# Preparing a scan block for two heads at once, with ScalarE placing the halves

## The chip, the core and the metric

The kernel runs on one core of a Trainium2 chip. Five engines work from their own instruction queues, each in order: TensorE (PE; its weight loads are PEld), VectorE (DVE), ScalarE (ACT), GpSimd (POOL) and SyncE (SP), which here issues all the DMAs. The metric is the time of one execution in device microseconds; before the change the median of three runs is 2986.44 us (2984.91 to 2988.6).

## The reference

The computation is three transformer layers in a row on one sequence of 512 tokens with 1024 channels, all in float32: neighbourhood attention with a gated convolution and an MLP, then a layer with RWKV-7 time mixing between two half-weighted SwiGLU blocks, then one with sliding-window attention between two more of them. The change touches only the RWKV-7 part, whose core is a recurrence over time, for each of 16 heads of 64 channels:

```
def step(S, inp):
    r_t, w_t, k_t, v_t, kk_t, b_t = inp
    sa = einsum('bhij,bhj->bhi', S, -kk_t)
    S = (S * w_t[:, :, None, :] + sa[..., None] * b_t[:, :, None, :]
         + v_t[..., None] * k_t[:, :, None, :])
    y = einsum('bhij,bhj->bhi', S, r_t)
    return S, y
```

Here kk is a normalised key, b = kk * a, and w the decay. The result y is normalised per head, gated and multiplied by an output matrix (w_o).

## The kernel before, in words

**Matrix products.** Every weight chunk of 128x1024 numbers is loaded by `wload` (line 406): a DMA on SP into a raw tile (wr, 3 buffers), a ScalarE copy to a rounded high part (wh, 5 buffers), and a subtraction on VectorE or GpSimd for the low part (wl, 5 buffers). TensorE multiplies three times: high by high, high by low, low by high. These products write PSUM tiles m; everything that runs beside them writes PSUM tiles t.

**The time-mixing part.** The tokens go in two halves, hf = 0 and 1. For each half the mixed inputs are multiplied in the order K (w_k), W, A (small matrices), R (w_r), V (w_v), G (small matrices), all of half 0 first, then of half 1. So the second w_k, w_r and w_v below are those of half 1. The results are spilled to DRAM.

**The scan.** The recurrence is cut into blocks of 128 tokens (j = 0 to 3, two chunks of 64 each), and the heads into two groups of eight, q = 0 and 1. Such a group lies as four pairs of heads in 128 partitions: head e = 0 of a pair in partitions 0 to 63, e = 1 in 64 to 127. For each of the 8 (q, j) there is a `prep(q, j)` (line 1358): it fetches five tiles from DRAM, builds the products of r and kk with the decay (tiles E, one for each e) and those of b and k with its inverse (tile bk), multiplies them on TensorE into small triangular matrices, and sends these (tile F) to DRAM (fsc). When both q of a block are prepared, `inverse(j)` (line 1451) reads them back (iat) and inverts them on GpSimd: 31 steps of a multiply and an add, one after the other (rows h<-a,iat and a<-a,h). The result is written to DRAM (xsc, line 1480) and read back, TensorE finishes the inverse with 32x32 products, and `scan_task(q)` (line 1577) runs the two chunks of the block. `gn_task` (line 1531) normalises a finished block, and `w_o(hf)` (line 1698) may start when both blocks of a half are normalised for both q: `em.until(lambda: min(done["z"]) >= 2 * hf + 1)`.

**What sets the order.** A planner, the class `_Emit`, keeps an estimated clock of every engine and runs these tasks as Python generators: each `yield` names tiles to wait for, and the task goes on when the estimate says that they are ready. So the program order on every engine follows from the estimates, and an instruction more or less moves those after it. A prep starts when at most one other is unfinished and when `room(12)` finds 12 free activation tiles of 56 (line 1524). SP issues its DMAs in this order too, and one that waits holds up those behind it.

**Lines.** The trace puts nearly all vector work on line 290 (292 where it is urgent), products on 379 and transposes on 393, so tile names tell it apart: a is an activation tile, h a half tile, s a small one, cst the constants, sv a state tile of the scan.

Of the kernel before, what the change touches and what calls it, by code (L numbers as in the profile page):

```python
# [297 lines left out]
def tile_net(ctx: ExitStack, tc: tile.TileContext, a: dict, out: bass.AP, dbg=None, stop=None):  # L298
# [13 lines left out]
    def nm(s):  # L312
        uid[0] += 1
        return f"{s}{uid[0]}"
# [3 lines left out]
    def A(dt=F32):  # L318
        live[0] += 1
        peak[0] = max(peak[0], live[0])  # L320
        t_ = apool.tile([P, T], dt, tag="a", name=nm("a"))
        em.new(t_, "a")
        return t_

    def free(*tiles, n=0):

        live[0] -= len(tiles) + n
        em.free(tiles, n)

    def room(n):  # L330
        return live[0] + n <= NA

    def S():
        return spool.tile([P, 64], F32, tag="s", name=nm("s"))

    def H():
        return HX()[:, 0:256]
# [4 lines left out]
    def PS(side=None):  # L342

        tag = "t" if (em.inside if side is None else side) else "m"
        t_ = psum.tile([P, T], F32, tag=tag, name=nm(tag), bufs=BANKS[tag])
        em.new(t_, tag)
        return t_
# [6 lines left out]
    vt, gp, act = _Engine(em, tc, nc.vector, "vt"), _Engine(em, tc, nc.gpsimd, "gp"), _Engine(em, tc, nc.scalar, "act")  # L354
    dma = _Engine(em, tc, nc.sync, "sync").dma_start
    MUL, ADD, SUB, MAX = ALU.mult, ALU.add, ALU.subtract, ALU.max
# [15 lines left out]
    def V(name, i=0):  # L372
        c = _VEC[name] + i
        return vec[:, c : c + 1]
# [3 lines left out]
    def mm(out_, lhsT, rhs, start=True, stop=True):  # L378
        nc.tensor.matmul(out_, lhsT=lhsT, rhs=rhs, start=start, stop=stop)  # L379
        n = 1  # L380
        for d in rhs.shape[1:]:
            n *= d
        m = lhsT.shape[-1]
        dur = 0.0134 * (1 if rhs.dtype == F32R else 2) + (max(n, 2 * m if m > 64 else m) if rhs.dtype == F32R else n * 4) / 2400.0
        em.pe(out_, [lhsT, rhs], em.tile_time(out_, lhsT, dur))
# [11 lines left out]
    def tt(eng, out_, in0, in1, op):  # L397
        eng.tensor_tensor(out=out_, in0=in0, in1=in1, op=op)

    def copy(out_, in_, scale=None):  # L400
        if scale is None:
            act.activation(out=out_, in_=in_, func=AF.Copy)
        else:
            act.activation(out=out_, in_=in_, func=AF.Copy, scale=scale)
# [76 lines left out]
    class Stat:  # L481
# [50 lines left out]
        def all(self):  # L532
            return self.ready[0] and self.ready[1]
# [28 lines left out]
    t_ = H()  # L562
# [76 lines left out]
    for j in range(4):  # L639
        t_ = A()  # L640
# [4 lines left out]
    for g in (1, 3, 5):  # L645
        t_ = A()
# [59 lines left out]
    with tc.tile_pool(name="bpool", bufs=4) as bias_p:  # L706
# [4 lines left out]
        for i in range(4):  # L711
            pc, ph = PS(), PS()
            gemm(pc, a["w_conv"], 3 * i, (0, 8), xs)
            t_ = A()
# [30 lines left out]
    for n in range(DC):  # L745
        sg = []
        for m in range(2):
            ps = PS()
            gemm(ps, a["w_gate"], 8 * m + n, (0, 8), xs)
            t_ = A()  # L750
# [11 lines left out]
        t_ = A()  # L762
# [3 lines left out]
    for c in range(DC):  # L766
        t_ = A()
# [317 lines left out]
    def fetch(src):  # L1085
        t_ = A()
        dma(out=t_, in_=src)
        return t_

    def fetch_q(d, q, j):  # L1090

        t_ = A()
        dma(out=t_.rearrange("p (q t) -> p q t", q=4),
                          in_=d[j // 2][4 * q : 4 * q + 4, :, (j % 2) * 128 : (j % 2 + 1) * 128].rearrange("q p t -> p q t"))
        return t_

    def rwkv(on_h):
# [245 lines left out]
        E, ARB, BKN, TT, PC, F = {}, {}, {}, {}, {}, {}  # L1343
# [14 lines left out]
        def prep(q, j):  # L1358
            kk, aa = fetch(kkd[q, j]), fetch_q(ad, q, j)
            k_, lg, r_ = fetch(kd_[q, j]), fetch(lgd[q, j]), fetch_q(rd, q, j)  # L1360
            yield [kk, aa]

            b_, k2 = A(), aa
            vt.scalar_tensor_tensor(out=b_, in0=kk, scalar=-1.0, in1=aa, op0=MUL, op1=MUL)
            for p in range(4):
                ps_ = slice(p * 128, (p + 1) * 128)
                act.activation(out=k2[:, ps_], in_=aa[:, ps_], func=AF.Identity, scale=V("k_a", 4 * q + p),
                               bias=oka[:, 4 * q + p : 4 * q + p + 1])
            tt(vt, k2, k2, k_, MUL)
            free(k_)  # L1370
            yield [lg, r_]
            ip, pp_ = A(), lg
            act.activation(out=ip, in_=lg, func=AF.Exp, scale=-1.0)
            act.activation(out=pp_, in_=lg, func=AF.Exp)
            pc = S()
            PC[q, j] = pc
            vt.tensor_copy(pc[:, 0:8].rearrange("p (q c) -> p q c", q=4),
                           pp_.rearrange("p (q c t) -> p q c t", q=4, c=2)[:, :, :, 63])

            def tv(t_, pr, c, x0=0, x1=64):  # L1380
                return t_.rearrange("p (q c t) -> p q c t", q=4, c=2)[pr, :, c, x0:x1]

            ff, rb_t = A(), A()
            F[q, j], ARB[q, j] = ff, rb_t
            f4 = ff.rearrange("p (c q f) -> p c q f", c=2, q=4)
            rb4 = rb_t.rearrange("p (c q f) -> p c q f", c=2, q=4)
            for c in range(2):
                bk, cg = A(), 2 * j + c
                b4 = bk.rearrange("p (q f) -> p q f", q=4)
                for e in range(2):  # L1390
                    pr = slice(64 * e, 64 * e + 64)
                    ee = A()
                    E[q, e, cg] = ee
                    e4 = ee.rearrange("p (q f) -> p q f", q=4)
                    tt(vt, e4[pr, :, 64:128], tv(r_, pr, c), tv(pp_, pr, c), MUL)
                    tt(vt, e4[pr, :, 1:64], tv(kk, pr, c, 1, 64), tv(pp_, pr, c, 0, 63), MUL)
                    copy(e4[pr, :, 0:1], tv(kk, pr, c, 0, 1))
                    ob, ok = (0, 64) if e == 0 else (64, 0)
                    tt(vt, b4[pr, :, ob : ob + 64], tv(b_, pr, c), tv(ip, pr, c), MUL)
                    tt(vt, b4[pr, :, ok : ok + 64], tv(k2, pr, c), tv(ip, pr, c), MUL)  # L1400
                    yield [k2,]
                yield (bk, *(E[q, e, cg] for e in range(2)))
                pas = [PS(), PS()]
                for p in range(4):
                    for e in range(2):
                        pr = slice(64 * e, 64 * e + 64)
                        mm(pas[e][:, p * 128 : (p + 1) * 128], bk[pr, p * 128 : (p + 1) * 128], E[q, e, cg][pr, p * 128 : (p + 1) * 128])
                for e in range(2):
                    pr, qr = slice(64 * e, 64 * e + 64), slice(64 - 64 * e, 128 - 64 * e)
                    ee = E[q, e, cg]  # L1410
                    p4 = pas[e].rearrange("p (q f) -> p q f", q=4)
                    copy(f4[pr, c], p4[pr, :, 0:64])
                    tt(vt, rb4[pr, c], p4[pr, :, 64:128], mA[pr, 64:128].unsqueeze(1).broadcast_to([64, 4, 64]), MUL)
                    tt(vt, ee.rearrange("p (q f) -> p q f", q=4)[qr], p4[qr], mA[qr].unsqueeze(1).broadcast_to([64, 4, 128]), MUL)
                pn = PS()
                for p in range(4):
                    transpose(pn[:, p * 128 : (p + 1) * 128], bk[:, p * 128 : (p + 1) * 128])
                BKN[q, cg] = A()
                copy(BKN[q, cg], pn)
                free(bk)  # L1420
            free(kk, b_, ip, pp_)
            f8 = ff.rearrange("p (u f) -> p u f", u=8)
            for e in range(2):
                for b in range(2):
                    r0 = 64 * e + 32 * b
                    dma(out=fsc[j].rearrange("b (q u e) (s t) -> b q e s u t", q=2, e=2, s=32)[b, q, e],
                        in_=f8[r0 : r0 + 32, :, 32 * b : 32 * b + 32])
            rk = A()
            for p in range(4):
                ps_ = slice(p * 128, (p + 1) * 128)  # L1430
                vt.scalar_tensor_tensor(out=rk[:, ps_], in0=r_[:, ps_], scalar=V("r_k", 4 * q + p), in1=k2[:, ps_], op0=MUL, op1=MUL)
            free(r_, k2)
            prepped[0] += 1
            if prepped[0] % 2 == 0:
                em.spawn(inverse(j))
            em.spawn(bonus(q, j, rk))
# [79 lines left out]
        prepped, scanned, inverted = [0], [0], [0]  # L1516

        def prep_task():
            for n in range(8):
                j, q = n // 2, n % 2  # L1520
                hf = j // 2
                while not all(flags.get(n_) for n_ in (("k", hf, q), ("lg", hf), ("a", hf), ("r", hf, q))):
                    yield 0.3
                while n >= prepped[0] + 2 or not room(12):
                    yield 0.3
                em.spawn(prep(q, j))
                yield 0.3
# [354 lines left out]
    for n in range(2):  # L1882
        t_ = A()
# [8 lines left out]
    for j in range(4):  # L1892
        t_ = kvpool.tile([P, 256], F32, name=nm("vsh"))
# [256 lines left out]
```

## Time and profile before

| what | value |
|---|---|
| median of 3 runs | 2986.44 us |
| profiled execution: its own time | 2986.91 us |
| profiled execution: span, first to last instruction | 2985.1 us |
| TensorE busy | 2820.6 us, 94% |
| VectorE busy | 1624.0 us, 54% |
| ScalarE busy | 1233.9 us, 41% |
| GpSimd busy | 692.3 us, 23% |
| mean granted TensorE clock | 0.968 |

TensorE is busy nearly all of the time, so the share of its idle time in a stretch, and the clock that it was granted there, tell where time can be won or lost. The preps run from about 1179 to 1536 us, beside the half-1 products, and the tables below cut that stretch into stages.

### The profile page before, as it was taken

The page shows a single profiled execution, that of the slowest core. Times are in us where ns is not written, and L with a number is a line of the kernel's source. Part 1 is how long each engine was busy: PE and PEld are TensorE (multiplying, and loading weights), DVE is VectorE, ACT ScalarE, POOL GpSimd, SP SyncE. Part 2 cuts the span into 40 slices and gives each one's busy share as a digit, 9 for nine tenths or more (in the row PEclk, how much of TensorE's full clock was granted, in tenths as well). Part 3 has the DMA queues.
Part 4 walks back from the last instruction along what each step waited for, and adds up shares of the span by engine and source line. Part 5 has one row for each costly group of instructions (what it writes and reads, how often), then busy time and mean ns, then how long its engine had stood idle before and what let it go on. Part 6 is the DMA issues. An engine that isn't in the chain of part 4 may idle for free. (4 is left out here: it accounts for less than half of the span.)

```text
span 2985.1 us, 45687 instructions
## 1 busy us (share of the span) xinstructions
PE 2820.6 (94%) x17736; PEld 2442.6 (82%) x17736; DVE 1624.0 (54%) x2896; ACT 1233.9 (41%) x2141; POOL 692.3 (23%) x802
## 2 busy tenths in 40 slices
PE   9999999999999989878789989998999989999998
PEld 7788888889888877656679989998888877888887
DVE  6545443335334486955676665366234476852336
ACT  4532333333333345544455544344233347733333
POOL 0022211111111143444355110111111134420111
PEclk9999999999999999988889999999999999999999
DMA  5333333332333455645565556343334432323334
GB/s 187 88 94 97 114 99 99 98 95 81 108 99 121 121 184 185 205 142 159 166 177 167 179 168 180 111 145 111 98 98 122 124 114 75 102 80 101 111 109 155
DMA packets 179408, 378.31 MB, mean 127 GB/s; under 512 B 57204, under 2 KB 81908, under 8 KB 179192
## 3 DMA queue, kind: packets, MB, share of 16 engines
q1 hardware_dynamic: 179192, 375.40, 41.6%
q8 instruction: 140, 2.29, 0.3%
q14 instruction: 76, 0.62, 0.1%
HBM read 342.04 MB, written 29.36 MB: 124 GB/s over the span
## 5 line engine op out<-in xcount | busy, mean ns | idle before, releaser
L379 PE MATMUL m<-a,wh 128*128 128x256 f32 (+1 forms) x8512 | 2061.5, 334 | 15.1 <-DVE a L290 7.2
L379 PEld LDWEIGHTS m<-a,wh 128*128 128x128 f32 x8512 | 1461.6, 192 | 178.7 <-issue 13.9
L379 PE MATMUL m<-a,wl 128*128 128x256 f32 (+1 forms) x4256 | 1414.1, 333 | 2.9 <-DVE wl L290 2.9
L290 ACT ACTIVATE wh<-wr 128x1024 fp32r<-128x1024 f32 (+2 forms) x585 | 606.0, 1038 | 1190.7 <-PE m L379 714.8
L290 DVE TENSOR_TENSOR wl<-wr,wh 128x1024 fp32r<-128x1024 f32 (+2 forms) x547 | 679.7, 1244 | 458.9 <-ACT wh L290 456.0
L379 PEld LDWEIGHTS m<-a,wl 128*128 128x128 f32 x4256 | 815.8, 192 | 78.4 <-DVE wl L290 3.5
L290 POOL TENSOR_TENSOR a<-a,a 128x256 f32<-128x256 f32 (+5 forms) x312 | 359.6, 1159 | 1633.5 <-ACT a L290 1317.4
L290 DVE TENSOR_TENSOR a<-m,a 128x512 f32<-128x512 f32 (+1 forms) x324 | 198.5, 614 | 629.6 <-PE m L379 618.9
L290 ACT ACTIVATE a<-a 128x512 f32<-128x512 f32 (+6 forms) x515 | 239.6, 481 | 121.3 <-DVE a L290 88.9
L379 PE MATMUL m<-wh,a 128*128 128x512 f32 x800 | 268.0, 409 | 12.5 <-DVE a L290 10.3
L379 PEld LDWEIGHTS m<-wh,a 128*128 128x128 f32 x800 | 155.7, 195 | 49.3 <-DVE a L290 12.5
L290 DVE TENSOR_TENSOR a<-a,a 128x256 f32<-128x256 f32 (+3 forms) x305 | 164.2, 567 | 36.0 <-ACT a L290 28.9
L379 PE MATMUL m<-wl,a 128*128 128x512 f32 x400 | 162.5, 406 | 0.0
L290 DVE SCALAR_TENSOR_TENSOR a<-a,vec,a 128x256 fp32r<-128x256 f32 (+4 forms) x246 | 144.9, 629 | 9.2 <-ACT a L290 8.4
L290 POOL TENSOR_TENSOR a<-h,a 128x256 fp32r<-128x256 f32 x80 | 68.3, 856 | 342.6 <-ACT a L290 328.0
L290 POOL TENSOR_TENSOR wl<-wr,wh 128x1024 fp32r<-128x1024 f32 x38 | 95.0, 2502 | 110.3 <-ACT wh L290 103.2
L379 PE MATMUL t<-a,a 64*128 64x128 f32 (+4 forms) x528 | 90.0, 356 | 32.0 <-DVE a L290 16.5
L379 PEld LDWEIGHTS t<-a,a 64*128 64x128 f32 (+3 forms) x528 | 57.4, 198 | 56.5 <-issue 25.6
L290 ACT ACTIVATE a<-t 128x512 f32<-128x512 f32 (+3 forms) x122 | 59.3, 491 | 90.0 <-PE t L379 70.6
L379 PEld LDWEIGHTS m<-wl,a 128*128 128x128 f32 x400 | 78.1, 195 | 16.1 <-issue 0.7
L290 ACT ACTIVATE a<-a,vec 128x256 fp32r<-128x256 f32 (+2 forms) x108 | 60.3, 565 | 47.2 <-DVE a L290 43.1
L292 ACT ACTIVATE a<-t 128x256 f32<-128x256 f32 (+3 forms) x100 | 45.4, 472 | 80.3 <-PE t L379 60.6
(108 smaller groups left out, 1533.5 us busy)
## 6 DMA issues: line engine op xcount, KB each, us to landing
wr<-in_ffn_w_in_dram SPq DMA_DIRECT2D x204, 512.0 KB, 3.7
wr<-in_ffn_w_out_dram SPq DMA_DIRECT2D x80, 448.0 KB, 3.3
wr<-in_ffn_w_out_dram SPq DMA_DIRECT2D x48, 512.0 KB, 3.6
wr<-in_w_out_t_dram SPq DMA_DIRECT2D x34, 512.0 KB, 3.7
wr<-in_w_mlp_in_dram SPq DMA_DIRECT2D x32, 512.0 KB, 3.6
wr<-in_w_mlp_out_dram SPq DMA_DIRECT2D x32, 512.0 KB, 3.7
wr<-in_w_gate_dram SPq DMA_DIRECT2D x16, 512.0 KB, 3.6
wr<-in_w_k_dram SPq DMA_DIRECT2D x16, 512.0 KB, 4.6
```

Source lines behind the costliest of these rows:

```text
L290: return fn(*args, **kw)
L292: return fn(*args, **kw)
L379: nc.tensor.matmul(out_, lhsT=lhsT, rhs=rhs, start=start, stop=stop)
```

## The change

The block preparation multiplies both heads of a pair in one instruction over 128 partitions, in place of one for each half of the partitions. The products of b and of k with the inverse decay are made once for the whole tile of both chunks (b in place, k in a new tile ki). As the bk tile wants the two products in a different order for the two heads, ScalarE copies each half to its place, four copies for a chunk; the E tile of head 1 gets its half by a fifth copy from that of head 0. The `yield` after each head goes, one stands ahead of the loop instead, and `room(12)` becomes `room(13)`.

```diff
+            ki = A()
+            tt(vt, b_, b_, ip, MUL)
+            tt(vt, ki, k2, ip, MUL)
+            free(ip)
+            yield [ki,]
+            both = slice(0, 128)
             for c in range(2):
-                bk, cg = A(), 2 * j + c
-                b4 = bk.rearrange("p (q f) -> p q f", q=4)
+                bk, e0, e1, cg = A(), A(), A(), 2 * j + c
+                E[q, 0, cg], E[q, 1, cg] = e0, e1
+                b4, e4 = (t_.rearrange("p (q f) -> p q f", q=4) for t_ in (bk, e0))
+                tt(vt, e4[:, :, 64:128], tv(r_, both, c), tv(pp_, both, c), MUL)
+                tt(vt, e4[:, :, 1:64], tv(kk, both, c, 1, 64), tv(pp_, both, c, 0, 63), MUL)
+                copy(e4[:, :, 0:1], tv(kk, both, c, 0, 1))
                 for e in range(2):
                     pr = slice(64 * e, 64 * e + 64)
-                    ee = A()
-                    E[q, e, cg] = ee
-                    e4 = ee.rearrange("p (q f) -> p q f", q=4)
-                    tt(vt, e4[pr, :, 64:128], tv(r_, pr, c), tv(pp_, pr, c), MUL)
-                    tt(vt, e4[pr, :, 1:64], tv(kk, pr, c, 1, 64), tv(pp_, pr, c, 0, 63), MUL)
-                    copy(e4[pr, :, 0:1], tv(kk, pr, c, 0, 1))
                     ob, ok = (0, 64) if e == 0 else (64, 0)
-                    tt(vt, b4[pr, :, ob : ob + 64], tv(b_, pr, c), tv(ip, pr, c), MUL)
-                    tt(vt, b4[pr, :, ok : ok + 64], tv(k2, pr, c), tv(ip, pr, c), MUL)
-                    yield [k2,]
+                    copy(b4[pr, :, ob : ob + 64], tv(b_, pr, c))
+                    copy(b4[pr, :, ok : ok + 64], tv(ki, pr, c))
+                copy(e1[64:128, :], e0[64:128, :])
                 yield (bk, *(E[q, e, cg] for e in range(2)))
...
-            free(kk, b_, ip, pp_)
+            free(kk, b_, ki, pp_)
...
-                while n >= prepped[0] + 2 or not room(12):
+                while n >= prepped[0] + 2 or not room(13):
```

Three places of the program order show what moves. The first is VectorE at the first prep's first chunk. Before:

```order
L290 COPY s_9508<-a_9414 128x8
L290 TENSOR_TENSOR a_9513<-a_9416,a_9414 64x4x64
L290 TENSOR_TENSOR a_9513<-a_9408,a_9414 64x4x63
L290 TENSOR_TENSOR a_9512<-a_9418,a_9505 64x4x64
L290 TENSOR_TENSOR a_9512<-a_9410,a_9505 64x4x64
L290 TENSOR_TENSOR a_9519<-a_9416,a_9414 64x4x64
L290 TENSOR_TENSOR a_9519<-a_9408,a_9414 64x4x63
L290 TENSOR_TENSOR a_9512<-a_9418,a_9505 64x4x64
L290 TENSOR_TENSOR a_9512<-a_9410,a_9505 64x4x64
L290 TENSOR_TENSOR wl_9595<-wr_9593,wh_9594 128x1024
```

and after the change:

```order
L290 TENSOR_TENSOR a_9418<-a_9418,a_9505 128x512
L290 TENSOR_TENSOR a_9410<-a_9410,a_9412 128x512
L290 SCALAR_TENSOR_TENSOR h_9551<-a_8440,vec 128x256
L290 COPY s_9508<-a_9414 128x8
L290 TENSOR_TENSOR a_9512<-a_9410,a_9505 128x512
L290 TENSOR_TENSOR a_9516<-a_9416,a_9414 128x4x64
L290 TENSOR_TENSOR a_9516<-a_9408,a_9414 128x4x63
L290 TENSOR_TENSOR wl_9596<-wr_9594,wh_9595 128x1024
```

Eight multiplies ahead of the weight split (wl) have become two of this chunk and two wide ones that serve the second chunk as well.

The second place is the SP queue where the first block's inverse goes to DRAM (xsc_8655), at the start of the second w_r. Before, prep 3's five fetches (from kkt_5532 to rd_5551) stand there, and the first w_r chunk comes behind xsc:

```order
L290 DMA a_10325<-kkt_5532 128x512
L290 DMA a_10327<-ad_5553 128x4x128
L290 DMA a_10329<-kt_5524 128x512
L290 DMA a_10331<-lg_5516 128x512
L290 DMA a_10333<-rd_5551 128x4x128
L290 DMA xsc_8655<-a_9976 32x16x32 x4
L290 DMA wr_10761<-in_w_r_dram 128x1024
L290 DMA sv_10850<-vd_5557 64x4x64
```

After the change:

```order
L290 DMA wr_10577<-in_w_r_dram 128x1024
L290 DMA bon_5544<-a_10203 128x512
...
L290 DMA a_10460<-in_a_dram 128x512
L290 DMA wr_10796<-in_w_r_dram 128x1024
L290 DMA sv_9600<-vd_5557 64x4x64
L290 DMA sv_10831<-vd_5557 64x4x64
L290 DMA sv_10952<-vd_5557 64x4x64 x2
L290 DMA sv_9603<-vd_5557 64x4x64
L290 DMA xsc_8655<-a_9967 32x16x32 x4
L290 DMA sv_9603<-vd_5557 64x4x64
L290 DMA wr_11039<-in_w_r_dram 128x1024
```

Two chunks of w_r have moved ahead of xsc; prep 3's fetches have left this place and stand 37 rows behind it (row 418 of the queue instead of row 373).

The third place is TensorE where the second block's inverse is finished (the first 32x32 product, of a_11631 before and of a_12117 now, which are read back from xsc). Before, it stands ahead of the second w_v, whose first three products follow:

```order
L379 MATMUL t_11635<-cst,a_11631 32x32 x16
L379 MATMUL t_11757<-h_11754,a_9923 32x32 x16
L393 MATMUL t_11663<-cst,a_11640 128x128 x4
L379 MATMUL t_11855<-a_11732,a_11731 128x128 x2
L379 MATMUL m_11797<-wh_11802,a_11775 128x512
L379 MATMUL m_11797<-wl_11803,a_11775 128x512
L379 MATMUL m_11797<-wh_11802,a_11775 128x512
```

After the change it stands behind the last product of w_v (first row), G's product (m_11986), the values' transposes and a chunk of prep 5 (t_12122, t_12123):

```order
L379 MATMUL m_11609<-wh_11931,a_11851 128x512
L379 MATMUL m_11986<-a_11866,a_11602 128x256 x2
...
L379 MATMUL t_12122<-a_12063,a_12062 128x128 x3
L379 MATMUL t_12123<-a_12064,a_12062 128x128 x3
...
L393 MATMUL t_12138<-cst,a_12062 128x128 x4
L379 MATMUL t_12093<-a_12087,a_12089 128x256
L379 MATMUL t_12160<-a_12087,a_12089 128x256
L379 MATMUL t_12121<-cst,a_12117 32x32 x16
```

So the second block's chain (32x32 products, two chunks of the scan for both q, normalisation) has moved from beside w_v to between w_v and the first w_o product, together with the first product groups of preps 5, 6 and 7.

## Rows read from the trace of the kernel before

**Rows 1.** The profile's page, first part: busy time of each engine.

```profile
PE 2820.6 (94%) x17736; PEld 2442.6 (82%) x17736; DVE 1624.0 (54%) x2896; ACT 1233.9 (41%) x2141; POOL 692.3 (23%) x802
```

**Rows 2.** Windows by stage, last the whole stretch (stretch, length, busy by engine, granted clock, DMA):

```profile
1186.00:1242.00 56.00, 42.91 (x217) 33.54 (x215) 53.65 (x92) 30.15 (x60) 24.59 (x20) 0.88 0.62 197
1279.00:1316.00 37.00, 19.31 (x77) 11.69 (x77) 24.15 (x52) 14.31 (x24) 11.21 (x21) 0.72 0.56 148
1382.00:1491.00 109.00, 81.86 (x767) 64.29 (x767) 73.73 (x168) 50.69 (x114) 33.78 (x48) 0.77 0.56 158
1491.00:1545.00 54.00, 45.86 (x414) 39.63 (x413) 41.07 (x91) 26.85 (x64) 21.78 (x41) 0.85 0.58 169
1186.00:1545.00 359.00, 287.16 (x2407) 228.02 (x2405) 252.55 (x507) 176.51 (x378) 160.90 (x255) 0.84 0.57 171
```

**Rows 3.** Waits of TensorE from 1186 to 1545 us (total, times, longest):

```profile
PE t L379 <- DVE a L290: 22.6, 12, 4.8
PE t L379 <- ACT a L290: 14.6, 2, 13.7
PE m L379 <- ACT a L290: 11.9, 3, 9.6
```

**Rows 4.** Groups by shape, whole span (busy us, mean ns | idle before):

```profile
L290 DVE TENSOR_TENSOR a<-a,a 64x256 f32<-64x256 f32 x96 | 43.6, 478 | 0.7 <-DMA bon<-a 0.2
L290 DVE TENSOR_TENSOR a<-a,a 64x252 f32<-64x252 f32 x32 | 21.4, 670 | 0.0
L290 DVE TENSOR_TENSOR a<-a,a 128x256 f32<-128x256 f32 x136 | 73.5, 552 | 14.2 <-ACT a L290 13.3
L290 DVE TENSOR_TENSOR a<-a,a 128x512 f32<-128x512 f32 x41 | 30.5, 743 | 21.1 <-ACT a L290 15.7 <-POOL a L290 4.4
L290 ACT ACTIVATE a<-a 64x4 f32<-64x4 f32 x32 | 6.5, 202 | 2.2 <-DMA bon<-a 1.8
L290 ACT ACTIVATE a<-t 64x256 f32<-64x256 f32 x32 | 12.0, 375 | 30.3 <-PE t L379 30.0
L290 ACT ACTIVATE a<-a 64x512 fp32r<-64x512 f32 x16 | 10.0, 627 | 0.4
```

**Rows 5.** Timeline, 1183 to 1204 us (start, length) of VectorE, GpSimd, TensorE:

```profile
1183.94 2.88 DVE L290 TENSOR_TENSOR a<-a,a 64x256 f32<-64x256 f32 x8
1197.65 5.00 DVE L290 TENSOR_TENSOR a<-a,a 64x256 f32<-64x256 f32 x8
1202.68 0.42 DVE L290 TENSOR_TENSOR a<-h,a 128x256 fp32r<-128x256 f32 x1
1199.09 2.60 POOL L290 TENSOR_TENSOR wl<-wr,wh 128x1024 fp32r<-128x1024 f32 x1 [4.51 <-DMA wr<-in_w_v_dram]
1203.16 1.22 PE L379 MATMUL m<-wh,a 128*128 128x512 f32 x2 [6.96 <-DVE a L290]
```

**Rows 6.** Groups by shape, 1186 to 1242 us only, VectorE:

```profile
L290 DVE TENSOR_TENSOR a<-a,a 64x256 f32<-64x256 f32 x26 | 11.2, 451 | 0.2
L290 DVE TENSOR_TENSOR a<-a,a 64x252 f32<-64x252 f32 x9 | 10.1, 1127 | 0.0
```

**Rows 7.** Waits of the SP queue, 1186 to 1545 us:

```profile
SPq L290 <- POOL a L290: 31.2, 3, 18.3
```

**Rows 8.** Timeline, 1285 to 1294 us, of SP queue, ScalarE, TensorE:

```profile
1285.24 1.95 SPq L290 DMA_DIRECT2D xsc<-a  x4
1287.23 0.51 SPq L290 DMA_DIRECT2D wr<-in_w_r_dram  x1
1293.61 2.66 PE L379 MATMUL t<-a,a 64*128 64x128 f32 x14 [13.71 <-ACT a L290]
```

**Rows 9.** Timeline of GpSimd and TensorE around the second block, 1381 to 1492 us:

```profile
1381.09 0.29 POOL L290 TENSOR_TENSOR a<-a,h 128x16 f32<-128x16 f32 x1
1391.40 0.69 PE L379 MATMUL t<-cst,a 32*32 32x32 f32 x32 [2.94 <-ACT a L292]
1491.07 1.20 PE L379 MATMUL m<-a,wh 128*128 128x256 f32 x4
```

## The prediction

> **What bounds the kernel now.** I read the page's first part, then windows by stage, TensorE's waits, the groups by shape, and the timeline around the longest waits. TensorE is busy for 94% of the span [rows 1], so over most of the program nothing that VectorE or ScalarE save can shorten it. The stretch where the preps run is the exception. From 1186 to 1545 us TensorE works 287.16 of 359 us and stands for 71.8 [rows 2]. The granted clock there is 0.84, against a mean of 0.968 for the whole execution, so it also spends part of the stretch at the lower level, 1.2 GHz in place of 2.4. VectorE is busy for 252.55 us of the stretch and ScalarE for 176.51, so ScalarE has the more room.
>
> The limits differ by stage [rows 2]. In the stage of the first w_v, 1186 to 1242, VectorE works 53.65 of 56 us: it is the bound, and TensorE stands for 13.1. At the second w_r, 1279 to 1316, TensorE works 19.31 of 37 us with no engine full: that is a wait for data. From 1382 to 1491, the second w_v and the end of block 1, TensorE stands for 27.1 us and its clock is 0.77. From 1491 to 1545 it stands for 8.1. These four hold 66 of the 71.8 us. In the list of waits VectorE's activation tiles hold TensorE 12 times for 22.6 us, ScalarE's twice for 14.6 and three times for 11.9 [rows 3].
>
> **The change part by part. The work.** Before, the eight preps issue 96 multiplies of 64x256 (43.6 us) and 32 of 64x252 (21.4 us), 65.0 in all [rows 4]. After, each prep has two of 128x512, two of 128x256 and two of 128x252. The first two kinds cost 743 and 552 ns [rows 4]; the third isn't in the trace, and I bound it by 552 ns (the 128x256) and 1127 ns (the slowest mean of the 64x252, [rows 6]), and take 670, its nearest row by element count. So 16 x 0.743 + 16 x 0.552 + 16 x 0.670 = 11.9 + 8.8 + 10.7 = 31.4 us: VectorE loses about 33 us (26 to 36 by the bounds). ScalarE drops 32 tiny copies at 202 ns and gets 16 of 128x4, taken at the same price (3.2 us less), 64 copies of 64x256 at 375 ns (a copy from PSUM, the nearest row, 24.0 us) and 16 of 64x512 at 627 ns (10.0 us) [rows 4]: about 31 us more. As 33 us leave one engine and 31 come to the other, the change is worth what VectorE's queue was holding up, less what ScalarE's will.
>
> Within one prep the way to the first product is about as long as before. It was eight multiplies at 0.36 us, 2.88 us [rows 5]. It is now two wide ones and two of one chunk, 2.7 us by the means above, and then five copies in a row on ScalarE, 4 x 0.375 + 0.627 = 2.1 us, of which those of the b and k halves can start beside the second pair of multiplies. Nothing is gained there for a prep alone; I set it at nothing, with 0 to +2 us a chunk for the bounds.
>
> At this place the profile has a second effect. The same eight multiplies took 2.88 us with GpSimd idle and 5.00 us while GpSimd ran a 2.60 us weight split beside them [rows 5]. The Trainium skill ("SBUF — State Buffer", section "SBUF: two separate sides") says that a VectorE operation with two SBUF inputs and a GpSimd operation that reads SBUF take a shared pair of ports in turn, one blocking while the other runs. The trace agrees: 5.00 less 2.88 is 2.1 us, near the split's 2.60. By that rule fewer and shorter multiplies would also hold up GpSimd's inverse less, on which B and C wait; if each of the 16 chunks met GpSimd's work and half of the 2.1 us went, that would be 17 us less at most, and the sum below between -15 and -32. By the rows alone, which show no inverse step that was held up, it is nothing, and nothing is what the sum has.
>
> **A, 1186 to 1242.** 35 of the old multiplies lie in this stage, 11.2 + 10.1 = 21.3 us [rows 6]. That is 2.2 preps, whose new form costs 2.2 x 3.9 = 8.6 us by the means, so VectorE gets back about 12 of its 53.65 us. One wait can be seen whole: a V-mix subtraction stood behind a chunk's eight multiplies, and TensorE waited 6.96 us for it [rows 5]. TensorE's idle time is 13.1 us, so the gain lies between 0 (ScalarE's copies hold up the weight copies instead) and 13.1; I take about the half, and the one visible wait: -7.
>
> **B, 1279 to 1316.** TensorE waits 13.71 us for a ScalarE tile, the weight's high part. It could not be made earlier because the DMA of w_r was issued at 1287.23, right behind that of xsc at 1285.24 [rows 8], and the SP queue had stood up to 18.3 us for GpSimd's inverse ahead of xsc [rows 7]. In the new order two w_r chunks stand ahead of xsc (the second place of the order above), so the wait should go. Late next is the third chunk, which still stands behind xsc. Bounds 0 and the stage's 17.7 us of idle time [rows 2]; I take -12, most of the 13.71.
>
> **C, 1382 to 1491.** Prep 3's fetches stand 37 rows further back on SP, so block 1's inverse starts later. Before, the inverse ended at 1381.09 and TensorE's first 32x32 product of it ran at 1391.40, beside w_v; the first w_o product, which needs that block's scan and normalisation, ran at 1491.07 [rows 9]. After, this chain stands behind the last product of w_v, and what it has beside it on TensorE is the first product groups of preps 5 to 7 alone. On SP, xsc of block 1 also stands ahead of fetches of prep 5 and of w_o's later chunks. The stage has 27.1 us of idle time already, so the bounds are -27.1 (all of it goes) and +27.1 (as much again is uncovered). VectorE has its share of the 33 us less here, 33 x 109/359 = 10 us, which speeds the chain's own vector work. I take +6: a quarter of the idle time more.
>
> **D, 1491 to 1545.** Preps 6 and 7 end here, with 41.07 us of VectorE work [rows 2]. A quarter of TensorE's 8.1 idle us goes, -2; bounds -8 and +8 (block 1's late products land here).
>
> **Sum.** -7 - 12 + 6 - 2 = -15. The profiled execution took 2986.91 us (its span 2985.1), 0.5 above the median of 2986.44, so it stands for the median: 2987 - 15 = 2972 us.
>
> **The rivals.** *R1, block 1's chain is bare (slower).* The place is between the last product of w_v and the first of w_o. If the chain starts behind w_v, time saved before it doesn't help, since w_o waits for the chain and not for w_v: A and B are absorbed. The stage's idle time doubles, +27.1, less VectorE's 10 us of relief: +17, 3004 us. For it: the order itself, and a clock already at 0.77, which further idling won't raise. Against it: the preps' products in the gap, and that B lets the queue run earlier. It decides once TensorE stands for more than some 45 us between those two products.
>
> *R2, the clock comes back (much faster).* A clock of 0.77 means 46% of the time at the lower level; of 81.86 busy us that is 37.7, half of which could be saved, 18.8. The same working gives 5.1, 5.4 and 6.9 us in the other three stages [rows 2], 36 in all. If less idle time in the stretch brings back some two thirds of that, it is -25 on top of -15: 2947 us. Against it: C adds idle time where most of it lies.
>
> *R3, no change.* ScalarE's copies of new weights queue behind up to 2.1 us of placing copies, and hold TensorE where VectorE did; and w_r's early chunks are followed by as long a wait for the third. A to D come to 0: 2987 us. For it: the one for one exchange of 33 against 31 us. Against it: ScalarE works only 49% of the stretch, 176.51 of 359.
>
> *R4, ScalarE is the wrong engine (slower).* There are 16 chunks, each with 2.1 us of copies in a row, 34 us. If ScalarE has other work that TensorE waits for as often as it is busy, 49%, that is 17 us of delay on weight copies and on the scan's evictions; A and D don't come: -12 + 6 + 17 = +11, 2998 us. The Trainium skill ("ScalarE: Activation LUTs", section "Rules for kernel authors") has simple elementwise work on VectorE rather than ScalarE, as that is up to about 3 times faster in bf16. In this trace, in float32, a ScalarE copy of 64x256 took 375 ns and a VectorE multiply of that shape 478, so for size the rows don't bear it out.
>
> **How the numbers follow.** The forecast has 0.40, R1 0.23, R2 0.15, R3 0.13, R4 0.09. By itself the forecast's terms give 2958 to 2981. The range has to take in half of R2 and half of R1, and all of R3 and R4: 2945 to 3005. About 0.2%, 6 us, is what a measurement of this kernel can tell from no change, so faster means below 2980.5 and slower above 2992.4. Faster: 0.38 of the forecast's 0.40, all of R2 and 0.01 of R3: 0.54. Within: the forecast's other 0.02 and 0.11 of R3: 0.13. Slower: R1, R4 and 0.01 of R3: 0.33.
>
> **What would show it right or wrong.** VectorE's busy time falls by about 33 us and ScalarE's rises by 31; if not, the work is mis-sized. A: in the stage of the first w_v VectorE is no longer above 90% busy, and the 6.96 us wait is gone. B: the 13.71 us wait at the second w_r is gone; if another of more than 8 us stands at the third chunk, R3 is right. C: the time from w_v's last product to w_o's first, and TensorE's idle time within it, tell it from R1. More waits on ScalarE's tiles in place of VectorE's point to R4, a granted clock above 0.84 in the stretch to R2. A time above 2992 would make the forecast wrong in C or D, one below 2958 in leaving out the clock.

## The result, and the profile after

The changed kernel takes 3013.11 us (median of four runs, 3012.97 to 3019.41), against 2987.09 for the kernel before beside it (four runs). The ratio is 1.0093, with a 95% interval of 1.0075 to 1.011: 26 us slower. The profiled execution has a span of 3011.2 us. All medians here are of undisturbed executions: one of a later run, which took 6134 us, is left out of its median.

The page's first part for the changed kernel, as [rows 1]:

```profile
PE 2819.9 (94%) x17736; PEld 2444.3 (81%) x17736; DVE 1602.6 (53%) x2816; ACT 1258.5 (42%) x2203; POOL 683.4 (23%) x802
```

VectorE works 21.4 us less and ScalarE 24.6 more; TensorE works as long as before, so the 26 us are time in which it stood (span less busy time: 191.3 us, where it was 164.5). The windows by stage, as [rows 2], with three more: 1316 to 1382, 1421.59 to 1520.47 (from the last product of w_v to the first of w_o) and 1545 to 1620:

```profile
1186.00:1242.00 56.00, 40.87 (x207) 32.03 (x207) 45.72 (x71) 37.00 (x80) 29.08 (x35) 0.85 0.61 197
1279.00:1316.00 37.00, 31.81 (x283) 21.60 (x284) 23.41 (x38) 22.59 (x47) 12.61 (x17) 0.87 0.61 187
1316.00:1382.00 66.00, 49.17 (x600) 42.40 (x600) 40.35 (x83) 36.16 (x79) 26.11 (x35) 0.89 0.72 208
1382.00:1491.00 109.00, 81.83 (x741) 64.38 (x742) 53.16 (x96) 55.99 (x128) 43.10 (x84) 0.74 0.45 134
1421.59:1520.47 98.88, 61.61 (x675) 49.38 (x675) 45.27 (x105) 49.58 (x116) 33.37 (x75) 0.68 0.56 164
1491.00:1545.00 54.00, 32.66 (x402) 28.39 (x403) 30.97 (x74) 26.16 (x63) 23.53 (x54) 0.78 0.47 132
1545.00:1620.00 75.00, 56.86 (x641) 52.85 (x634) 53.69 (x120) 32.80 (x66) 40.54 (x69) 0.84 0.50 145
1186.00:1545.00 359.00, 268.42 (x2379) 213.82 (x2380) 218.07 (x399) 194.48 (x427) 159.74 (x264) 0.83 0.55 167
```

The kernel before has, for the three that [rows 2] lacks:

```profile
1316.00:1382.00 66.00, 62.11 (x766) 51.46 (x765) 28.55 (x54) 37.35 (x79) 42.95 (x77) 0.90 0.55 178
1465.10:1491.07 25.97, 12.94 (x58) 10.88 (x59) 14.66 (x45) 16.35 (x35) 12.34 (x29) 0.68 0.78 240
1545.00:1620.00 75.00, 71.14 (x838) 67.31 (x835) 60.49 (x117) 43.00 (x88) 55.77 (x84) 0.97 0.63 175
```

From 1279 to 1316 TensorE now works 31.81 us where it worked 19.31: the 13.71 us wait is gone. From 1382 to 1491 it works as long as before, 81.83 us. It works less from 1316 to 1382 (49.17 us where it was 62.11), from 1491 to 1545 (32.66 where it was 45.86) and from 1545 to 1620 (56.86 where it was 71.14). Between w_v and w_o it stands for 37.3 of 98.9 us, where it stood for 13.0 of 26.0. Over the whole stretch to 1700 us the number of products done, in brackets behind TensorE's busy time, says how far the program has come. The kernel before and the changed one:

```profile
1186.00:1700.00 514.00, 436.74 (x4188) 370.30 (x4187) 358.79 (x705) 264.11 (x547) 229.26 (x350) 0.88 0.58 172
```

```profile
1186.00:1700.00 514.00, 403.66 (x3929) 341.44 (x3929) 316.85 (x601) 272.07 (x583) 212.74 (x345) 0.85 0.53 160
```

259 products are still to be done at 1700 us that had been done before, and TensorE has stood for 33 us more. At 403.66 / 3929 = 0.10 us a product, an estimate over products of all sizes, that is about the 26 us: the loss lies between 1186 and 1700.

Where, the timeline shows. SP's queue from the first block's xsc on (the transfer ahead of it, xsc, prep 3's first fetch, the result of the second block's inverse going out, a transfer that waits, and the read back):

```profile
1265.56 3.22 SPq L290 DMA_DIRECT2D sv<-vd  x5
1282.17 1.97 SPq L290 DMA_DIRECT2D xsc<-a  x4
...
1325.46 0.44 SPq L290 DMA_DIRECT2D a<-kkt  x1
...
1413.56 1.96 SPq L290 DMA_DIRECT2D xsc<-a  x4
...
1424.12 4.33 SPq L290 DMA_DIRECT2D vd<-a  x4
...
1438.49 1.44 SPq L290 DMA_DIRECT2D a<-xsc  x2
```

The same three of the second block in the kernel before (fetch, result, read back), and its last product of w_v:

```profile
1264.44 0.38 SPq L290 DMA_DIRECT2D a<-kkt  x1
...
1381.41 1.96 SPq L290 DMA_DIRECT2D xsc<-a  x4
...
1386.00 1.04 SPq L290 DMA_DIRECT2D a<-xsc  x2
...
1464.70 0.40 PE L379 MATMUL m<-wh,a 128*128 128x512 f32 x1
```

SP stood 13.4 us ahead of the first block's xsc (1268.78 to 1282.17). So of the 61 us by which prep 3's fetch is later, xsc itself took the smaller part; the other 41 us, from 1284 to 1325, are the rows that stand between.

GpSimd's last step of the second block's inverse in the changed kernel, and TensorE from its first product on the result to the first w_o product (answering [rows 9]):

```profile
1413.30 0.23 POOL L290 TENSOR_TENSOR a<-a,h 128x16 f32<-128x16 f32 x1
...
1421.20 0.39 PE L379 MATMUL m<-wh,a 128*128 128x512 f32 x1
...
1444.23 1.06 PE L379 MATMUL t<-cst,a 32*32 32x32 f32 x32 [0.25 <-ACT a L290]
...
1508.58 1.11 PE L393 MATMUL t<-cst,a 128*128 128x128 f32 x4 [14.99 <-POOL a L292]
...
1516.05 2.87 PE L379 MATMUL t<-a,a 64*128 64x128 f32 x16 [6.35 <-DVE s L292]
...
1520.47 1.24 PE L379 MATMUL m<-a,wh 128*128 128x256 f32 x5
```

The row at 1421.20 is the last product of the second w_v. From there to the first w_o product are 99 us. Before, the inverse ended at 1381.09, its products began at 1391.40 and w_o at 1491.07 [rows 9]; now these are 1413.30, 1444.23 and 1520.47, so 32, 53 and 29 us later. The longest waits in the gap, 14.99 and 6.35 us, are for the normalisation's steps on GpSimd and VectorE, which stand one after the other with nothing for TensorE beside them. The SP rows add that the read back was issued 25 us after xsc (1438.49 - 1413.56; 1386.00 - 1381.41 = 5 us before), behind prep 5's fetches, chunks of w_o and transfers of w_v's results such as the 4.33 us one.

The waits of TensorE, as [rows 3]:

```profile
PE t L393 <- POOL a L292: 26.7, 3, 15.0
PE m L379 <- ACT a L290: 15.1, 3, 7.7
...
PE t L379 <- ACT a L290: 7.9, 5, 4.0
...
PE t L379 <- DVE a L290: 5.9, 1, 5.9
```

The waits of the t products for VectorE's tiles have gone from 22.6 us to 5.9 and the 13.7 us one for ScalarE is gone too. The normalisation (line 292) has taken their place.

The groups by shape, as [rows 4]:

```profile
L290 DVE TENSOR_TENSOR a<-a,a 128x256 f32<-128x256 f32 x152 | 83.5, 559 | 15.8 <-ACT a L290 15.0
L290 ACT ACTIVATE a<-a 64x256 f32<-64x256 f32 x64 | 23.1, 405 | 1.6 <-DVE a L290 1.2
L290 DVE TENSOR_TENSOR a<-a,a 128x512 f32<-128x512 f32 x57 | 39.2, 694 | 13.0 <-ACT a L290 7.5 <-POOL a L290 4.4
L290 ACT ACTIVATE a<-a 64x512 f32<-64x512 f32 x16 | 10.0, 623 | 19.5 <-DVE a L290 16.0 <-issue 2.5 <-ACT a L290 0.8
L290 DVE TENSOR_TENSOR a<-a,a 128x252 f32<-128x252 f32 x16 | 7.4, 463 | 0.0
```

The new multiplies cost (83.5 - 73.5) + (39.2 - 30.5) + 7.4 = 26.1 us, against 65.0 [rows 4]. ScalarE's copies cost 23.1 + 10.0 + 3.2 - 6.5 = 29.8 us more than before (the 3.2 us are the 16 of 128x4).

### The profile page after: what moved, and what is told of

It reads as the page before. It is cut to its first block, busy times and chain, and to the rows that moved or that the text cites. A ratio compares the mean times of both kernels' runs of the same rounds, so it can differ in the third digit from the quotient of the medians.

```text
span 3011.2 us, 45690 instructions
## 1 busy us (share of the span) xinstructions
PE 2819.9 (94%) x17736; PEld 2444.3 (81%) x17736; DVE 1602.6 (53%) x2816; ACT 1258.5 (42%) x2203; POOL 683.4 (23%) x802
## 5 line engine op out<-in xcount | busy, mean ns | idle before, releaser
L290 ACT ACTIVATE a<-a 128x256 f32<-128x256 f32 (+7 forms) x579 | 268.9, 484 | 142.9 <-DVE a L290 115.2
L290 DVE TENSOR_TENSOR a<-a,a 128x256 f32<-128x256 f32 (+2 forms) x225 | 128.8, 586 | 28.8 <-ACT a L290 22.5
L393 PE MATMUL t<-cst,a 128*128 128x128 f32 x256 | 44.2, 312 | 38.6 <-POOL a L292 32.3
```

Of the source, the lines that this page charges most:

```text
L290: return fn(*args, **kw)
L393: nc.tensor.transpose(out_, in_, ident[: in_.shape[0], : in_.shape[0]])
```

## The experiments

Two theories stood at the start. The first: the loss is prep 3's late start. `room(13)` held it back until tiles came free, its fetches fell behind the first block's xsc on SP, and everything of block 1 came late. The second: ScalarE's copies are what costs. A third, that any change of order costs about so much, was the control. Five rounds were run of each kernel; the kernel before, beside them, had medians of 2986.6 to 2988.0 us.

**One number, both ways.** The changed kernel with prep 3 alone let in earlier:

```diff
-                while n >= prepped[0] + 2 or not room(13):
+                while n >= prepped[0] + 2 or not room(12 if n == 3 else 13):
```

> The changed kernel, with room(12) in place of room(13) for prep 3 alone; all the new multiplies and copies stay. In its program order prep 3's fetches stand ahead of the first block's xsc again, as before the change. Theory 1 (the loss is prep 3's late start, which delays block 1's inverse and so w_o): the first w_o product starts near 1490 us in place of 1520, TensorE's bare stretch ahead of it shrinks from some 96 us to under 50, and the time is 2975 to 2990. Rival 2 (the copies on ScalarE are what costs): w_o may move, but the time stays within 8 us of 3013. Rival 3 (any change of order costs about so much): 3000 to 3020.

Measured: 2982.26 us, ratio to the kernel before 0.9987 (0.9978 to 0.9996).

```profile
1261.89 0.44 SPq L290 DMA_DIRECT2D a<-kkt  x1
...
1471.92 0.84 PE L379 MATMUL m<-a,wh 128*128 128x256 f32 x4 [0.32 <-ACT a L292]
```

Prep 3's first fetch is 64 us earlier, w_o 49 us, and the loss is gone with every new multiply and copy in place. The bare stretch between w_v's last product (at 1435.08) and w_o is 37 us in place of 99, as the first theory had it. The reverse, on the kernel before: `room(13 if n == 3 else 12)`.

> The kernel before, with room(13) for prep 3 alone: old multiplies, no copies on ScalarE; only prep 3 starts late, its fetches behind the first block's xsc. Theory 1: as slow as the changed kernel or slower, 3005 to 3030, with w_o starting 25 to 40 us later than 1491. Rival 2: within 8 us of 2987.

Measured: 3006.8 us, 1.0064 (1.0052 to 1.0076).

```profile
1327.94 1.60 SPq L290 DMA_DIRECT2D a<-kkt  x1
...
1514.39 0.51 PE L379 MATMUL m<-a,wh 128*128 128x256 f32 x2
```

The old work is 19 us slower when prep 3's fetch moves from 1264 to 1328; w_o moves from 1491 to 1514, 23 us and not the 25 to 40 expected. As in the changed kernel TensorE stood (190.0 us of the span, where it was 164.5). The place is another: w_v's last product is itself late here, at 1481.94, and the idle time grew from 1382 to 1491 (37.1 us where it was 27.1) and from 1545 to 1620 (16.1 where it was 3.9). The first theory holds in both directions. The second explains neither run. The third, that any change of order costs, is against the first run and those below that change the order and are faster.

**The number for all preps.** The changed kernel with `room(12)`, and the kernel before with `room(13)`.

> The changed kernel with room(12) for all preps, as before the change. Theory 1: as the first run, 2970 to 2990; if VectorE's 39 us less of multiplies are worth anything beside the order, it is below 2987. Rival 2: within 8 us of 3013.

Measured: 2971.89 us, 0.9951 (0.9939 to 0.9963). The change without its new limit is 15.6 us faster than before.

```profile
1260.92 0.44 SPq L290 DMA_DIRECT2D a<-kkt  x1
...
1469.45 1.44 PE L379 MATMUL m<-a,wh 128*128 128x256 f32 x5 [1.17 <-ACT a L292]
```

> The kernel before with room(13) for all preps: the one number of the change alone. In its order prep 2 starts a little later and prep 3 earlier than with 12, so theory 1 (what counts is when prep 3 starts, not the number) expects 2975 to 2995. If the number 13 is bad by itself: 3005 to 3020.

Measured: 2984.8 us, 0.9988 (0.998 to 0.9997). The number is not harmful by itself. Prep 3's fetch is at 1230.80 here, ahead of the first block's xsc at 1303.55.

> The changed kernel with room(11): prep 3's fetches stand at row 345 of the SP queue, against 371 with room(12) and 418 with room(13). If earlier is still better: 2960 to 2970. If only a late start harms, and what comes before its products is hidden: 2968 to 2978, the same as with 12.

Measured (the changed kernel with `room(11)`): 2972.69 us, 0.995 (0.9938 to 0.9962), the same as with 12. Starting prep 3 some 25 us earlier still, at 1236, gains nothing.

**The halves of the change**, on the kernel before with `room(12)`. First the b and k products alone (the wide multiplies, ki and the four copies a chunk).

> The kernel before with the b and k part of the change alone: wide multiplies with the inverse decay and four placing copies a chunk on ScalarE; r and kk with the decay as before, head by head; room(12). Prep 3's fetches stand ahead of xsc as before (row 373). Theory 1: not slow, 2965 to 2990. If VectorE's saved time is worth what it takes less of (some 18 of the 39 us), about half of the third run's gain: 2976 to 2984.

Measured: 2979.46 us, 0.9979 (0.9969 to 0.9989). Then the products of r and kk with the decay alone, where only one copy a chunk goes to ScalarE:

```diff
-                    tt(vt, e4[pr, :, 64:128], tv(r_, pr, c), tv(pp_, pr, c), MUL)
-                    tt(vt, e4[pr, :, 1:64], tv(kk, pr, c, 1, 64), tv(pp_, pr, c, 0, 63), MUL)
+                tt(vt, e4[:, :, 64:128], tv(r_, both, c), tv(pp_, both, c), MUL)
+                tt(vt, e4[:, :, 1:64], tv(kk, both, c, 1, 64), tv(pp_, both, c, 0, 63), MUL)
...
+                        copy(e1[64:128, :], e0[64:128, :])
```

> The kernel before with the r and kk part alone: one multiply for both heads, and head 1's half copied by ScalarE; b and k as before; room(12). Prep 3 starts well before the first block's xsc (row 339 of the SP queue against 390). Theory 1: 2965 to 2990; by VectorE's saved time (some 21 us), 2974 to 2984. If starting prep 3 even earlier than before helps w_o: below 2972.

Measured: 2967.0 us, 0.9936 (0.9922 to 0.995), faster than the whole change with 12, and below the 2974 to 2984 that went by VectorE's saved time. So the half with 10 us of copies gains 20 us and the half with 23 us of copies gains 8. The orders differ too (prep 3's fetch is at 1223 in the one and at 1267 in the other), so this is no price of the copies.

**Where the copies run.** In the changed kernel with `room(12)` all the placing copies as `vt.tensor_copy`.

> The changed kernel with room(12) and all placing copies on VectorE in place of ScalarE. Theory 1 (the order sets the time, prep 3 is early): 2968 to 2990. If ScalarE's copies cost in the third run (2971.89), this is below 2968; if what VectorE was relieved of made that run's gain, it is 2980 to 2992.

Measured: 2977.56 us, 0.9965 (0.9953 to 0.9978), 6 us slower than with ScalarE's copies. Prep 3 started at 1232 here and not at 1261, so the orders differ and the 6 us are not a price of the engine. The Trainium skill's advice on elementwise work ("ScalarE: Activation LUTs", section "Rules for kernel authors") names relu, max, min, add and mul. For a float32 copy, which it doesn't name, this run agrees in kind: VectorE's of 64x256 took 338 ns, ScalarE's in the changed kernel 405.

**What the work is worth at one order.** So far each run also changed the order. In the next two the planner counted what it had counted before, so the program keeps the order of the kernel before but for a few per cent of SP's DMAs. First, each of the 128 multiplies became a shorter copy:

```diff
-                    tt(vt, b4[pr, :, ob : ob + 64], tv(b_, pr, c), tv(ip, pr, c), MUL)
+                    light(b4[pr, :, ob : ob + 64], tv(ip, pr, c), tv(b_, pr, c))
...
+        def light(out_, in0, in1):
+            em.op("vt", "tensor_tensor", [out_], [in0, in1])
+            vt.eng.tensor_copy(out_, in1)
```

> The kernel before, its program order all but kept: each of the 128 prep multiplies is a plain copy of one operand on VectorE, which is shorter, while the planner still counts a multiply. It leaves out the products with the decay. This prices VectorE's relief alone, at the old order and without ScalarE's copies. If VectorE was the bound where the prediction's step A put it: 5 to 15 us faster, 2972 to 2982. If TensorE's waits there are on the chain of the preps and not on VectorE's load: within 4 us of 2987.

Measured: 2964.87 us, 0.9932 (0.9915 to 0.9949).

```profile
L1360 DVE COPY a<-a 64x256 f32<-64x256 f32 x96 | 34.0, 381 | 0.5
...
L1360 DVE COPY a<-a 64x252 f32<-64x252 f32 x32 | 9.5, 298 | 0.0
```

By these sums VectorE was relieved of 65.0 - 43.5 = 21.5 us, by its busy time of 13.2 (1624.0 to 1610.8), and the kernel became 21.7 us faster (medians of the same runs, 2986.57 less 2964.87): more than either side expected. That 21.7 is near 21.5 does not make VectorE the bound of step A, whose stage has little of it: from 1186 to 1242 TensorE stands for 11.5 us in place of 13.1. w_o starts 18 us earlier, at 1473.22. Then ScalarE's 80 copies were added, unknown to the planner.

> The run with lighter VectorE work, and besides, on ScalarE, the placing copies of the change (64 of 64x256 and 16 of 64x512, each of a tile onto itself), unknown to the planner. It leaves out the same products. This is the changed work at the old order. If the copies are hidden, as ScalarE works only half of the stretch: within 4 us of the run without them. If they cost what they take on the way to the preps' products (16 chunks of about 2.1 us): 10 to 30 us slower than that run.

Measured: 2999.6 us, 1.0045 (1.0031 to 1.0058): 35 us slower than the run before it, for 33 us of copies. TensorE's longest entry in the list of waits (1186 to 1640 us) is theirs:

```profile
PE t L379 <- ACT a L1406: 23.1, 7, 9.5
```

The cost is a little more than the second of the two expectations allowed, but little of it is TensorE standing longer. The page's first parts, without the copies and with them:

```profile
PE 2809.1 (95%) x17736; PEld 2433.5 (82%) x17736; DVE 1610.8 (54%) x2896; ACT 1235.2 (42%) x2141; POOL 691.9 (23%) x802
PE 2837.0 (95%) x17736; PEld 2452.5 (82%) x17736; DVE 1602.9 (53%) x2896; ACT 1264.5 (42%) x2221; POOL 691.4 (23%) x802
```

The spans are 2965.2 and 2997.5 us, so TensorE stood for 156.1 and 160.5 us, and was busy 27.9 us longer with the same 17736 products. Its granted clock from 1186 to 1700 was 0.91 without the copies and 0.87 with them. So the copies moved TensorE's waits, and most of what they cost came as longer busy time at a lower clock. What brought the clock down was not tried. The gain of the run without them splits in the same way: against the kernel before TensorE was busy 11.5 us less (2820.6 to 2809.1) and stood 8.4 us less. With the copies known to the planner:

> The lighter VectorE work plus the placing copies, with the copies now counted by the planner, which may put other products between them and the preps' products. It leaves out the products with the decay. If what the planner knows hides the copies: 2960 to 2978, close to the run without them (2964.87). If they cost their own time wherever they stand, as the preps are a chain: 2990 to 3005.

Measured: 2987.54 us, 0.9998 (0.9988 to 1.0008), which neither side expected. With each run taken against its own runs of the kernel before, the planner's knowledge took some 13 of the 35 us off; 21 stay. The order is another here, and TensorE's busy time, 2840.2 us, is the longest of all the runs.

**The same fault at another prep.** The r and kk half with `room(13)` and with `room(11)`:

> The r and kk part alone, with room(13) in place of 12. Prep 3's fetches stand well ahead of the first block's xsc with either number, so the number shouldn't matter: 2960 to 2980. If 13 is harmful whatever the tiles do: over 3000.

Measured: 2997.34 us, 1.004 (1.0026 to 1.0053). A miss: 30 us slower than with 12, though prep 3's fetch is at 1233, ahead of the first block's xsc.

> The r and kk part alone, with room(11). Prep 3 starts later than with 12 but still ahead of the first block's xsc. If each step earlier of prep 3 is worth something: 2972 to 2980, against 2967 with 12. If only a start behind xsc harms: 2960 to 2975.

Measured: 2964.83 us, 0.9933 (0.9919 to 0.9948), the best of all the runs, though not distinct from the run with 12. Prep 3's fetch is at 1264.57 here and at 1222.95 with 12, so its early start is not what the half gained by. With 13, prep 4's fetches had come to stand behind the second block's xsc. So prep 4 alone was let in earlier (`room(12 if n == 4 else 13)`), and alone held back (`room(13 if n == 4 else 12)`).

> The r and kk part with room(13) for all preps but prep 4, which has 12. Prep 4's fetches stand ahead of the second block's xsc again. If a prep whose fetches wait behind an xsc is what costs: 2960 to 2975, as with 12 for all. If something else in the order with 13 costs: 2990 to 3003.

Measured: 2973.79 us, 0.9951 (0.9933 to 0.9969).

```profile
1347.44 0.43 SPq L290 DMA_DIRECT2D a<-kkt  x1
...
1363.94 0.33 SPq L290 DMA_DIRECT2D xsc<-a  x1
```

> The r and kk part with room(12) for all preps but prep 4, which has 13. Prep 4's fetches stand behind the second block's xsc (row 454 of the SP queue against 444). If that is what costs: 2985 to 3003. If not: 2960 to 2975.

Measured: 2992.07 us, 1.0018 (1.0005 to 1.0031).

```profile
1366.06 1.96 SPq L290 DMA_DIRECT2D xsc<-a  x4
...
1376.21 0.60 SPq L290 DMA_DIRECT2D a<-kkt  x1
```

Prep 4's fetch at 1347, ahead of xsc: fast. At 1376, behind it: 25 us slower than with 12 for all. So the fault has nothing to do with prep 3 itself: the preps are a chain that feeds one inverse after another, and one that starts late makes its block's inverse late. In the profiled executions, 32.1 us apart, 9.7 us of the loss are TensorE standing longer and 22.4 its longer busy time (2806.2 with 12 for all, 2828.6 with prep 4 late).

A place behind xsc does not cost by itself. The kernel before with `room(13)` has prep 4's fetch behind xsc too (1383 against 1375) and is not slower. The date at which the third block's inverse goes out, which preps 4 and 5 feed, fits: it is no later there than in the kernel before (first row, then the kernel before):

```profile
1516.61 1.96 SPq L290 DMA_DIRECT2D xsc<-a  x4
1520.00 0.32 SPq L290 DMA_DIRECT2D xsc<-a  x1
```

Prep 5's fetch had come earlier, at 1392 where it was 1425. With the r and kk half this xsc is at 1492 and 1494 in the runs with 11 and 12 for all, at 1502 where prep 4 alone had 12, and at 1515 in both slow ones. The date of the second block's xsc goes with the time in the same way where only the limits were changed: 1366 for the changed kernel with 12, 1369 with 12 for prep 3, 1414 as it was; 1381 for the kernel before, 1408 with prep 3 late. This is a reading of the traces, and the cause in that one case stays open: no run moved an xsc alone.

## Why the prediction was wrong

It forecast 2972 us, 15 faster, and the kernel is 26 slower. The time lies past the range's upper end of 3005.

**The work** was right in kind and off in size. The multiplies were to fall from 65.0 to 31.4 us and fell to 26.1, as the 128x252 took 463 ns and not 670 and the wide ones 39.2 - 30.5 = 8.7 us and not 11.9. ScalarE's 31 us were 29.8. But VectorE's busy time fell by 21.4 us and not by 33. Two things lie between: other VectorE work became longer (all its durations together fell by 26.8 us, from 1738.4 to 1711.6, where these groups fell by 38.9), and neighbouring instructions overlap in the trace (the eight multiplies of 0.40 to 0.43 us each, 3.3 us in sum, stood in 2.88 us [rows 5]).

By the stages of the sum, TensorE's idle time changed so: A's +2.0 us, B's -12.5, C's 0.0, D's +13.2. Outside them it rose by 3.0 from 1242 to 1279, by 12.9 from 1316 to 1382, and by 14.3 from 1545 to 1620, where the sum did not look.

**A** (-7) was wrong. VectorE fell from 53.65 to 45.72 busy us in the stage, but TensorE's work there fell too. The wait of 6.96 us was replaced by one of 5.93 ahead of a prep's own products (first row below), and one for a ScalarE tile grew from 2.0 to 7.7 us. The bound of 0 had allowed for such a wait; that the placing copies made it is not shown.

```profile
1195.94 1.62 PE L379 MATMUL t<-a,a 64*128 64x128 f32 x6 [5.93 <-DVE a L290]
...
1294.15 0.50 PE L379 MATMUL m<-a,wh 128*128 128x256 f32 x2
```

**B** (-12) was right in its stage: w_r's first products run at 1294 with no wait ahead (second row), and 12.5 us more TensorE work is done in the same time. It misread the wait. The row of 13.71 us is ahead of a prep's products (t<-a,a), and they waited for copies of 64x4 that stood in ScalarE's queue, at 1293.36, behind the rounding of w_r, which waited for its DMA:

```profile
1291.79 1.06 ACT L290 ACTIVATE wh<-wr 128x1024 fp32r<-128x1024 f32 x1 [12.06 <-DMA wr<-in_w_r_dram]
```

So w_r's DMA was the cause, as B said. In the changed kernel another wait stands there, 8.84 us for a VectorE tile up to 1283.88. And from 1316 to 1382 TensorE stood 12.9 us more, about what B had gained.

**C** (+6) is the step that failed. The order in the document showed prep 3's fetches 37 rows further back and block 1's chain behind w_v. The prediction put a share of one stage's idle time on that, a quarter, where it should have followed the date: a fetch 61 us later (1264 to 1325), an xsc 32 us later, a read back 52 us later, w_o 29 us later. The stage itself, 1382 to 1491, has no more idle time than before (27.2 us, 27.1 before); the cost lies behind it, 13.2 us from 1491 to 1545 and 14.3 from 1545 to 1620. w_v finished earlier by some 43 us (its last product stood at 1465 before and stands at 1421), which gained nothing, since w_o waits for the chain. This is the mechanism of rival R1: A and B absorbed. Its sign did not come, as TensorE stood for 37 us between the two products and not for more than 45. Its price of +17 was too low: it doubled the idle time of a stage that did not change, and had neither the stretch behind 1545 nor the 20 us more that the read back stood in SP's queue.

**D** (-2) went with C: TensorE's idle time from 1491 to 1545 rose from 8.1 to 21.3 us, past the bound of +8.

**The shared ports**, which the sum had at nothing: the 248 steps of the inverse on GpSimd took 116.8 us in all before, 110.8 in the changed kernel and 120.1 in it with `room(12)`, so no run shows a gain there near 17 us.

**R2, R3, R4.** The clock did not come back in the changed kernel (0.83 against 0.84 in the stretch), but in other runs R2's mechanism is seen: TensorE was busy 14.4 us less with the r and kk half (2806.2) and 11.5 less with the lighter multiplies. R4 does not explain this loss, as the first experiment with all copies in place shows, but its price was not too high: at or near the old order the copies cost 21 to 35 us, more than the 17 it gave, and for the most part as longer busy time of TensorE and not by the waits that it named.

With `room(12)` the changed kernel takes 2971.89 us, the forecast to the microsecond. That is no merit of the sum: the prediction was for the kernel with 13, and its terms were not the ones that made this time.

## What to carry to other kernels

Where a planner or a limit on buffers sets the order, a change of a limit by one can move a whole task, and its price is read from the date at which the next stage's last input now arrives, followed row by row, not from a share of idle time. In a queue that works in order, look for the fetch that has moved back behind a transfer which waits for a slow engine, and then for whether the next result is later for it. Moving work to an engine that is half idle wasn't free here, where that work is a link of the chain that the bound engine waits for. And split a difference into the time that the bound engine stood and the time that it was busy with the same work: here the second was longer where the granted clock was lower.

## What had not been expected of the hardware

A multiply over 128 partitions took hardly longer than one over 64 of the same length: 559 against 478 ns for 256 elements a partition, as means of the whole span, and 409 against 451 from 1186 to 1242. For 252 elements the means of whole runs spread more than the two shapes differ: 444 to 683 ns over 128 partitions, 518 to 670 over 64. And shorter work on VectorE changed how long TensorE was busy with the same 17736 products: with the lighter multiplies the granted clock from 1186 to 1700 rose from 0.88 to 0.91 and the busy time fell by 11.5 us. With the late prep 3 the clock fell to 0.85, but the busy time did not rise; there TensorE stood.
